# One encoder layer in emulated fp32: output and down projections with stationary weights and features on partitions

## The chip, the core and the metric

The kernel is written in Bass with the Tile framework and runs on one core of a Trainium2 chip. The time is device microseconds of one execution; the profile is one execution taken by the hardware profiler.

A core has five engines with instruction queues of their own: PE (matrix products; its weight loads are counted apart as PEld), DVE, ACT and POOL (elementwise work) and SP (here it only issues transfers). An engine takes its instructions in order and waits for semaphores of the others. Transfers between DRAM and the on-chip memory run on 16 DMA engines. On-chip tiles have 128 partitions. PE multiplies a stationary operand of at most 128 x 128 by a moving operand and writes into PSUM; "128x272" behind a matmul is its output, 128 partitions by 272 moving columns.

## What is computed

One inference step of one layer: 1024 prompt frames and 64 sample frames, each with 1024 features. The two parts share all weights, so the kernel treats them as T = 1088 tokens.

```python
def trunk(x, ...):
    m = mixer(rmsnorm(x, g_mix), ...)       # projection, conv and attention, gates, w_out
    x = x + m
    x = x + swiglu(rmsnorm(x, g_ffn), w_ff1, w_ff3, w_ff2)
    return rmsnorm(x, g_final)

def mixer(xn, ...):
    cb, cc, ch, q, k, v, ga, gb = split(xn @ w_in)      # 1024 x 5120
    ya = (cb * conv3(cc * ch)) @ w_conv_out
    yb = band_attention(q, k, v) @ w_attn_out
    return (sigmoid(ga) * ya + sigmoid(gb) * yb) @ w_out   # 1024 x 1024

def swiglu(x, w1, w3, w2):                  # 1024 x 2816, twice, then 2816 x 1024
    return (silu(x @ w1) * (x @ w3)) @ w2

def rmsnorm(x, g):                          # over the features of a token
    return x * rsqrt(mean(x * x) + 1e-6) * g
```

## The kernel before

**Numbers.** An fp32 operand is held as two parts of PE's fast fp32 type: `hi`, a cast on ACT, and `lo = x - hi` on DVE (`split`, lines 152 and 153). A product of two operands is three matmuls: hi·hi, hi·lo, lo·hi.

**Seven products.** The input projection, the up-projection (w_ff1 and w_ff3) and the down-projection (w_ff2) use a seven-product scheme of 2 x 2 blocks. The moving operand is kept as seven tiles 1 to 7, each a block of tokens and features or a sum of blocks (class `Seven`). `first` builds tiles 1 and 2 from the first token half; `second` builds 3 to 7 from the second half and from what was kept of the first. `both` is a split, `minus` a difference on DVE (line 160). The products run in the order `STEPS = [1, 2, 6, 7, 5, 4, 3]`. A `Unit` is 256 columns of a weight; `prep(step)` makes its part on ACT and DVE, `step_of` (`sa_step`, `sb_step` for the first two units) issues the products of one step.

**Columns.** A half is HT = 544 token columns (512 prompt tokens and 32 sample frames), HN = 272 is half of that. In the layouts with features on partitions the columns are prompt tokens 0 to 511, 32 sample frames, prompt tokens 512 to 1023, 32 sample frames.

**Stages.** V projection (0 to 78 us), the rest of the input projection (to 373), attention and gates (to 573), merge of the two branches (to 671), output projection (to about 782), up-projection (to 1239), down-projection (to 1473), end. The Tile framework schedules each engine's list ahead of time from the program and its dependences; a pool's buffers come free tile by tile, and `tc.issue_after` sets an instruction behind another.

**Output projection** (lines 1061 to 1225). The merged input `mg` has features on partitions, in four tiles of half the features by half the tokens (tiles 1 to 4 of the up-projection later overwrite it). In `token_product` 128 tokens of `mg` are stationary and 512 columns of w_out move, so that tokens come out on partitions: 8 groups of 128 prompt tokens, and the 64 sample frames, which have a copy `ms` with hi and lo side by side. The first output half (`wo_hi`, `wo_lo`) adds the residual, stores the sums x1 and x1 times g_ffn, and takes the row sum of squares from ACT's accumulation. The second half (`second`) goes in `ORDER = [8, 0, 4, 1, 5, 2, 3, 6, 7]`: add, square, a factor of one column (`norm_factor`, lines 162 to 171: scale, Sqrt, reciprocal, a Newton step), two scaled halves (the first half read back, on ACT; the second on DVE, L1174). `turned` (L1176) transposes the token group on PE, in eight 128 x 128 pieces, and calls `xf.first` or `xf.second`. It runs one group late; the last group's stands between the up-projection's first steps.

**Hidden layer** (`hidden_done`). The product silu(a)·b is split into hi and lo and stored in seven tiles (`h_d`); its sample frames go apart (`hs_d`).

**Down-projection** (lines 1268 to 1590). 128 tokens of a hidden tile are stationary (`ht`), 512 columns of w_ff2 move from a ring of prepared weights (`Down`, `W2`, `ring_of`). The hidden features go in four blocks (KB = 2, 3, 3, 3 pairs of tiles), within one two token groups g, seven steps, two pieces j. PSUM tags: A, two buffers of one bank; BD, four of one. The 64 sample frames are multiplied without the scheme, in `frames`, into PSUM of their own (`ys`). In the last block the residual is added, and `half_ended` (L1468) works per 128 tokens: squares with accumulation, `norm_factor`, two scaled halves with a row of g_final (`gfb`; L1490), stores of 128 tokens by 512 features by SP and ACT.

Of the kernel before, what the change touches and what calls it, by code (L numbers as in the profile page):

```python
# [15 lines left out]
P = 128  # L16
# [26 lines left out]
def spots(a, n):  # L43


    edges = [(0, 512, 0), (512, 1024, 544)]
    r = []
    for lo, hi, at in edges:
        s, e = max(a, lo), min(a + n, hi)
        if s < e:  # L50
            r.append((s - a, at + s - lo, e - s))
    return r
# [42 lines left out]
def encoder_kernel(ctx: ExitStack, tc: tile.TileContext, ins, outs):  # L95
# [23 lines left out]
    cols = const.tile([P, 20], F32, name="cols")  # L119
    nc.scalar.dma_start(cols, ins["cols"])  # L120
    gm = cols[:, 12:20]
# [4 lines left out]
    x1_d = dr.tile([T, D], F32, name="x1_d")  # L126
    y0_d = dr.tile([T, 512], F32, name="y0_d")
    h_d = dr.tile([NF // 2, 7, P, 4 * 2 * P], F32, name="h_d")
    hs_d = dr.tile([NF // 2, P, 2, 2 * TS], F32, name="hs_d")
# [43 lines left out]
    class Seven:  # L173
# [5 lines left out]
        def first(self, src, c, n, kept=None):  # L179
            for g in range(2):  # L180
                both(self.t[1 + g], c, n, src[g])
                if kept is not None:
                    act.copy(kept[:, g], src[g])

        def second(self, src, c, n, kept, f):
            t = self.t
            both(t[3], c, n, src[1])
            minus(f[:, 0], src[0], kept[:, 0])
            minus(f[:, 1], src[1], f[:, 0])
            both(t[6], c, n, f[:, 1])  # L190
# [70 lines left out]
    def bank2(tag, nm):  # L261
        return stage["ps"].tile([P, 2, 512], F32, tag=tag, name=nm, bufs=2 if tag == "A" else 1)
# [112 lines left out]
    HORDER = [0, 1, 2, 8, 4, 3, 5, 6, 7]  # L375
    with tc.tile_pool(name="ph", bufs=2, reuse_waits="tile") as ph:
        xts, xns, pls = {}, {}, {}

        def load_x(i):
# [3 lines left out]
            xt = xts[i] = ph.tile([P, KD, P], F32, tag="xt", name=f"xt{i}", bufs=6)  # L383
# [47 lines left out]
        def formed(i):  # L431
# [8 lines left out]
            if i == 8:  # L440
# [96 lines left out]
    def conv_units(cvp, c2):  # L537
# [44 lines left out]
        def cb_done(r, h, src, snap):  # L582
# [4 lines left out]
            for a, t, n in places(h):  # L587
                nc.gpsimd.dma_start(u_d[i * P : (i + 1) * P, t : t + n], x[:, a : a + n])
# [6 lines left out]
    def cache_tile(hp):  # L595
        ct = cp.tile([P, CACHE], F32, tag="ct", name=f"ct{hp}")
# [108 lines left out]
    gp = pool_of("gp", 3, stack=t_stack)  # L705
# [14 lines left out]
    def gate_chunk(n, c, behind=None):  # L720
# [74 lines left out]
    def row_sums(h):  # L795
# [8 lines left out]
        nc.gpsimd.dma_start(r_d[h, :TP].rearrange("(a p) -> a p", p=P), rr[:8])  # L804
        nc.gpsimd.dma_start(r_d[h : h + 1, TP:], rr[8:9, :TS])

    def combine(h, pv, n, tok, nm):
# [7 lines left out]
        nc.gpsimd.dma_start(o_d[h * HD : (h + 1) * HD, tok : tok + n], o[:, :n])  # L815
# [148 lines left out]
    pm_stack.close()  # L964
    o_stack.close()
# [13 lines left out]
    ms = mspool.tile([P, KD, 2, TS], F32R, tag="ms", name="ms")  # L979
# [27 lines left out]
    with tc.tile_pool(name="mgp", bufs=3, reuse_waits="tile") as mp:  # L1007
        for m0 in range(0, 8, 2):
            for j in range(2):
# [26 lines left out]
                def joined(c):  # L1036
# [5 lines left out]
                    if o + n > TP:  # L1042
                        split(ms[:, m, 0, :], ms[:, m, 1, :], t[:, TP - o : n])
# [13 lines left out]
    t_stack.close()  # L1057
# [568 lines left out]
```

## Time and profile before

| what | value |
|---|---|
| median of three runs | 1484.99 us (1484.95 to 1487.14) |
| the profiled execution | 1482.88 us, its span 1481.1 us |
| mean granted PE clock | 0.998 |
| read from and written to DRAM | 170.56 MB and 87.62 MB, 174 GB/s |
| matmuls on PE in windows: input projection (78 to 373 us) | 2326 |
| merge and output projection (573 to 782 us) | 1115 |
| up-projection (782 to 1239 us) | 3652 |
| down-projection (1239 to 1473 us) | 1036 |

The span runs from the first to the last instruction; the execution's own time has 1.8 us more. The page gives busy time of each engine, the span in slices, the chain of work that ended last, and groups of instructions by source line. In a group's row stand line, engine and operation, output<-inputs, shape, count, then busy us and mean ns of one, then idle time of the engine ahead of them and what ended most of it. Matmuls overlap in the array, so that a group's mean is longer than the time from one start to the next. In the views by windows a row has the stretch, its length, busy time (and count) of PE, PEld, DVE, ACT and POOL, the granted clock, the share of time that the DMA engines were busy, and GB/s.

### The profile page before, as it was taken

The page shows a single profiled execution, that of the slowest core. Times are in us where ns is not written, and L with a number is a line of the kernel's source. Part 1 is how long each engine was busy: PE and PEld are TensorE (multiplying, and loading weights), DVE is VectorE, ACT ScalarE, POOL GpSimd, SP SyncE. Part 2 cuts the span into 40 slices and gives each one's busy share as a digit, 9 for nine tenths or more (in the row PEclk, how much of TensorE's full clock was granted, in tenths as well). Part 3 has the DMA queues.
Part 4 walks back from the last instruction along what each step waited for, and adds up shares of the span by engine and source line. Part 5 has one row for each costly group of instructions (what it writes and reads, how often), then busy time and mean ns, then how long its engine had stood idle before and what let it go on. Part 6 is the DMA issues. An engine that isn't in the chain of part 4 may idle for free.

```text
span 1481.1 us, 25804 instructions
## 1 busy us (share of the span) xinstructions
PE 1460.2 (99%) x9864; PEld 1366.2 (92%) x9864; DVE 1001.7 (68%) x1962; ACT 680.2 (46%) x1383; POOL 198.1 (13%) x347
## 2 busy tenths in 40 slices
PE   8999999999999999999999999999999999999997
PEld 6799999999999999998889999999999999888886
DVE  7976565653577776755688667766666667957676
ACT  6544332322677775642465444444344445512223
POOL 0344221122122221001100111111001111000000
PEclk9999999999999999999999999999999999999999
DMA  9666332346766627636533444343334448867675
GB/s 312 197 225 216 133 63 85 65 133 202 209 172 176 172 79 214 204 116 224 167 97 124 154 153 148 145 160 124 114 127 161 146 171 302 305 210 248 207 265 201
DMA packets 144876, 256.48 MB, mean 173 GB/s; under 512 B 20288, under 2 KB 84096, under 8 KB 144608
## 3 DMA queue, kind: packets, MB, share of 16 engines
q1 hardware_dynamic: 116720, 169.56, 37.2%
q0 software_dynamic: 26736, 83.17, 15.7%
q10 hardware_dynamic: 1296, 2.11, 0.4%
q8 instruction: 77, 1.26, 0.4%
q14 instruction: 47, 0.39, 0.1%
HBM read 170.56 MB, written 87.62 MB: 174 GB/s over the span
## 4 chain that ended last, share of the span: by engine, by line
PE 94%; DVE 2%; ACT 2%; DMA 1%; issue 1%; POOL 0%; SPq 0%; ACTq 0%; DVEq 0%; POOLq 0%
PE Aa L285 9%; PE Ab L285 9%; PE A L1541 8%; PE Db L285 4%; PE Da L285 4%; PE D L1541 4%; PE Ag L285 3%; PE p L701 2%; PE p L699 2%; PE p L700 2%; PE t L863 2%; PE Bb L285 2%; PE Ba L285 2%; PE B L1541 2%; PE wo L1078 2%; PE wo L1079 2%
## 5 line engine op out<-in xcount | busy, mean ns | idle before, releaser
L1541 PE MATMUL A<-ring,ht 128*128 128x512 f32 x528 | 124.4, 390 | 0.0
L1541 PEld LDWEIGHTS A<-ring,ht 128*128 128x128 f32 x528 | 99.0, 188 | 21.1 <-ACT acc L1551 0.2
L1261 POOL DMA_DIRECT2D h_d<-hq x77 | 41.1, 534 | 406.7 <-DVE hq L153 207.8
L152 ACT CAST ring<-w2r 128x512 fp32r<-128x512 f32 (+1 forms) x78 | 43.2, 588 | 88.6 <-PE A L1541 42.7
L152 ACT CAST hq<-sa 128x512 fp32r<-128x512 f32 x77 | 47.8, 621 | 75.0 <-DVE sa L1273 56.8
L153 DVE TENSOR_TENSOR wla<-rawa,wha 128x512 fp32r<-128x512 f32 x55 | 37.8, 688 | 42.7 <-ACT wha L152 42.7
L153 DVE TENSOR_TENSOR hq<-sa,hq 128x512 fp32r<-128x512 f32 x77 | 53.0, 689 | 20.0 <-ACT hq L152 19.9
L1541 PE MATMUL D<-ring,ht 128*128 128x512 f32 x264 | 63.4, 392 | 0.0
L1541 PEld LDWEIGHTS D<-ring,ht 128*128 128x128 f32 x264 | 49.6, 188 | 11.1
L783 DVE CUSTOM_DVE_ANT_0 p<-s,bias 128x640 f32<-128x640 f32 (+5 forms) x72 | 47.4, 659 | 17.3 <-PE s L833 17.2
L285 PE MATMUL Aa<-tt,wha 128*128 128x272 f32 x352 | 58.8, 288 | 0.1
L285 PE MATMUL Ab<-tt,whb 128*128 128x272 f32 x352 | 58.6, 287 | 0.0
L285 PE MATMUL Ab<-mg,whb 128*128 128x272 f32 x352 | 58.4, 288 | 0.0
L285 PE MATMUL Aa<-mg,wha 128*128 128x272 f32 x352 | 58.4, 288 | 0.0
L152 ACT CAST wha<-rawa 128x512 fp32r<-128x512 f32 x55 | 33.9, 621 | 51.3 <-PE Ab L285 36.0
L701 PE MATMUL p<-xo,wlp 128*128 128x272 f32 x192 | 57.0, 297 | 0.0
L700 PE MATMUL p<-xo,whp 128*128 128x272 f32 x192 | 56.4, 294 | 0.0
L699 PE MATMUL p<-xo,whp 128*128 128x272 f32 x192 | 56.2, 293 | 0.0
L153 DVE TENSOR_TENSOR ring<-w2r,ring 128x512 fp32r<-128x512 f32 (+1 forms) x78 | 48.4, 647 | 11.3 <-ACT ring L152 11.3
L793 ACT ACTIVATE p<-p,mx 128x640 f32<-128x640 f32 (+5 forms) x72 | 50.9, 706 | 9.2 <-DVE mx L783 8.7
L152 ACT CAST whb<-rawb 128x512 fp32r<-128x512 f32 x55 | 34.0, 620 | 39.4 <-PE Aa L285 26.8
L1553 DVE TENSOR_TENSOR acc<-A,acc 128x512 f32<-128x512 f32 x52 | 35.7, 687 | 23.3 <-PE A L1541 22.9
(523 smaller groups left out, 4557.7 us busy)
## 6 DMA issues: line engine op xcount, KB each, us to landing
h_d<-hq POOLq DMA_DIRECT2D x77, 512.0 KB, 3.8
ht<-h_d SPq DMA_DIRECT2D x154, 256.0 KB, 3.5
rawa<-in_w_ff SPq DMA_DIRECT2D x11, 1024.0 KB, 6.0
rawb<-in_w_ff SPq DMA_DIRECT2D x11, 1024.0 KB, 5.2
w2r<-in_w_ff SPq DMA_DIRECT2D x11, 1024.0 KB, 7.1
qd<-q_d SPq DMA_DIRECT2D x32, 272.0 KB, 5.5
xn<-in_x_prompt SPq DMA_DIRECT2D x8, 512.0 KB, 6.7
xt<-in_xt SPq DMA_DIRECT2D x8, 512.0 KB, 6.1
```

The costliest lines, as they stand in the source:

```text
L152: c = act.copy(hi, src)
L153: vec.tensor_tensor(lo, src, hi.bitcast(F32), op=ALU.subtract)
L285: mm(t[:, j, :HN], x[:, k, :], moving(p, l, k, j * HN, HN), start=p in (1, 2, 7) and k == 0 and n == 0, stop=k == 3 and n == 2, skip_group ...
L699: mm(out, a, p, start=g == 0 and k == 0, stop=False)
L700: mm(out, a, q, start=False, stop=False)
L701: mm(out, b, p, start=False, stop=g == last and k == 3)
L783: vec.tensor_tensor_reduce(out=s if len(ps.shape) == 2 else s.rearrange("p (a b) -> p a b", a=2), in0=ps, in1=bias if len(ps.shape) == 2 e ...
L793: act.activation(s, s, AF.Exp, bias=mx, scale=-1.0, accum_out=sm)
L863: nc.tensor.transpose(tp[:, i * P : (i + 1) * P], s[:, i * P : (i + 1) * P], ident)
L1261: nc.gpsimd.dma_start(h_d[p, c - 1], hq.rearrange("p i l t -> p (i l t)").bitcast(F32))
L1541: mm(t, ht[k][:, j, x], w[:, l], start=p in (1, 2, 7) and k == 0 and n == 0, stop=k == len(ks) - 1 and n == 2, skip_group_check=p in (6, 5 ...
L1553: behind["DVE"] = vec.tensor_tensor(o, t, o, op=ALU.add).ins
```

## The change

Tokens no longer come out on partitions anywhere.

**Output projection.** `projected(hf, c)` takes one output half hf and one of four chunks c of 272 token columns; weights are stationary (128 x 128), `mg` moves, and 128 features by 272 tokens come out. Chunks 0 and 1 are the first token half. `PASS` sets the order: 0, 1, 2, 3 for the first output half, 0, 2, 1, 3 for the second. Squares are taken by ACT with features on partitions, added on DVE, and summed over partitions by an f32 product with a matrix of -0.5 (`rows2`), which leaves the same row on all partitions. `row_factors` turns that 128 x 272 row into factors with the operations that were done on one column before. The scaling multiplies by a column of g_ffn and by that row, 272 columns at a time. The sums x1 are stored features first and the first half of them is read back (`half_load`); the input x comes transposed from the host's copy. There are no transposes, no `y0_d`, no `ms`. The seven tiles are built in pieces of 272 instead of 128 columns; `both` is at lines 149 and 150 and `minus` at 157 now.

**Down-projection.** Weights are stationary, `ht` moves 272 columns; the sample frames are in the columns, so `frames`, `hs_d` and `ys` go. PSUM: A and BD have two buffers of two banks. `ended` replaces `half_ended`: squares are added up over the four pieces of a chunk, summed by a product with -0.5, turned into factors, and eight scaled products and four stores per chunk follow. The output leaves as one array `y`, features by 1088 columns, and the host takes it apart. The residual's rows are loaded into free parts of the weight ring.

**Elsewhere.** Gates, conv outputs, attention outputs and their factors are stored in the 1088-column order, so a piece of 544 goes with one store where two went. The merge's pieces split at columns 544 instead of 512. The tile order at the start (`HORDER`) goes from 0, 1, 2, 8, 4, 3, 5, 6, 7 to 0, 1, 4, 2, 5, 8, 3, 6, 7; the buffers of `xt` from 6 to 5 and of `ct` to 1; one pool moves to the other side of memory. In the up-projection's first two units the steps stand in another order (below), and their PSUM for B and D has two buffers instead of one.

```diff
+    def projected(hf, c, weights):
...
+        for mp in range(2):
+            t = bank2("A", f"wo{hf}{c}{mp}")
+            for j in range(2):
+                w = slice((2 * mp + j) * P, (2 * mp + j + 1) * P)
+                for k in range(KD):
+                    wh, wl = weights(k)
+                    for n, (a, l) in enumerate(((wh, 0), (wh, 1), (wl, 0))):
+                        mm(
+                            t[:, j, :HN], a[:, w], mg.at(l, k, c * HN, HN),
...
+            y = x[:, 2 * mp : 2 * mp + 2]
+            added = vec.tensor_tensor(y, t[:, :, :HN], y, op=ALU.add).ins
+            squared = act.activation((q, r)[mp], y, AF.Square).ins
...
+        rows = bank2("BD", f"rows2_{c}")[:, 0, :HN]
+        mm(rows, minus_half, q[:, 0], start=True, stop=True)
...
+    def row_factors(pool, rows, nm):
...
+        vec.tensor_scalar(v, rows, -2.0 / D, EPS, op0=ALU.mult, op1=ALU.add)
+        act.activation(y, v, AF.Sqrt)
+        vec.reciprocal(y, y)
+        act.activation(z, y, AF.Square)
+        vec.tensor_tensor(z, z, v, op=ALU.mult)
+        vec.scalar_tensor_tensor(z, z, -3.0, y, op0=ALU.add, op1=ALU.mult)
...
+    def second(n):
+        c = PASS[1][n]
...
+        x, rows = projected(1, c, lambda k: w2[k])
+        r = row_factors(wp, rows, f"f{c}")
+        src = [first_x.pop(c), x]
+        for g in range(2):
+            for m in range(4):
+                y = src[g][:, m]
+                at = 4 * g + m
+                vec.scalar_tensor_tensor(y, y, g_neg[:, at : at + 1], r, op0=ALU.mult, op1=ALU.mult)
+        if c < 2:
+            kept[c] = src
+            xf.first(src, c * HN, HN)
+        else:
+            xf.second(src, (c - 2) * HN, HN, kept.pop(c - 2), src)
...
     sa_step(0)
     sa_step(1)
-    turned(*last)
...
     sb_step(0)
     sb_step(1)
+    sa_step(2)
     for si in range(2, len(STEPS)):
+        ub.prep(si)
+    sb_step(2)
+    for si in range(3, len(STEPS)):
         sa_step(si)
-        ub.prep(si)
+    for si in range(3, len(STEPS)):
+        sb_step(si)
...
+                    for j in range(2):
+                        c = slice((2 * jp + j) * P, (2 * jp + j + 1) * P)
+                        for k, kp in enumerate(ks):
+                            w = W2[kp].w[p]
+                            for n, (l, x) in enumerate(((0, 0), (0, 1), (1, 0))):
+                                mm(
+                                    t[:, j, :HN], w[:, l, c], ht[k][:, x],
```

In the whole program PE's matmuls go from 9857 to 10962: those of 272 columns from 6816 to 9443, those of 512 from 1750 to 324. DVE's instructions go from 1964 to 1863, ACT's from 1278 to 1156.

The first place is the end of the output projection on PE. Before, the last token group's 512-column products (`wo_7`) are followed by another group's transposes and the first step of the up-projection (`Aa`; `wha` and `wla` are the parts of its weights, `mg_7065` is tile 1):

```order
L1077 MATMUL wo_7_8939<-woh_7_8423,mg_7068 128x512
L1078 MATMUL wo_7_8939<-wol_7_8424,mg_7068 128x512
L1079 MATMUL wo_7_8939<-woh_7_8423,mg_7068 128x512
L1191 MATMUL xt_6_8976<-ident,xg_6_8878 128x128 x8
L285 MATMUL Aa_9011<-mg_7065,wha_1_8461 128x272 x4
L285 MATMUL Aa_9011<-mg_7065,wla_1_8462 128x272 x2
L285 MATMUL Aa_9011<-mg_7065,wha_1_8461 128x272 x4
L285 MATMUL Aa_9011<-mg_7065,wla_1_8462 128x272 x2
```

Now the last chunk's products of 272 columns are followed by the product over partitions of the chunk ahead of it, and then by the up-projection's first products on tile 1 (`mg_7032`), which alternate between the first unit (`Aa`) and the second (`Ab`):

```order
L1125 MATMUL wo_9016<-mg_7035,woh_7_8535 128x272 x2
L1125 MATMUL wo_9016<-mg_7035,wol_7_8536 128x272
L1142 MATMUL rows_1_8940<-q_8832,minus_half 128x272
L280 MATMUL Aa_9113<-mg_7032,wha_1_8546 128x272
L280 MATMUL Ab_9196<-mg_7032,whb_1_9105 128x272
L280 MATMUL Aa_9113<-mg_7032,wha_1_8546 128x272 x2
L280 MATMUL Ab_9196<-mg_7032,whb_1_9105 128x272 x2
L280 MATMUL Aa_9113<-mg_7032,wha_1_8546 128x272
L280 MATMUL Aa_9113<-mg_7032,wla_1_8547 128x272 x2
```

So no transposes stand between them any more, and the up-projection's first step comes behind two chunks of which the last has no row product yet.

The second place is DVE in the second output half. Before, between the add-back of one token group (`wo_5`) and its scaled product stand the lo parts and sums of an earlier group, in pieces of 512 elements, and factors of one column:

```order
L1095 TENSOR_TENSOR x_5_8701<-wo_5_8703,x_5_8701 128x512
L153 TENSOR_TENSOR tt_8456<-left_8627,tt_8456 128x4x128
L153 TENSOR_TENSOR mg_7067<-left_8627,mg_7067 128x4x128
L166 TENSOR_SCALAR normf_8732<-ssq_5_8730,more 128x1
L153 TENSOR_TENSOR mg_7065<-xt_1_8740,mg_7065 128x4x128
L168 RECIPROCAL normf_8732<-normf_8732 128x1
L169 SCALAR_TENSOR_TENSOR normf_8732<-normf_8732 128x1
L170 SCALAR_TENSOR_TENSOR normf_8732<-normf_8732 128x1
L1174 SCALAR_TENSOR_TENSOR xg_5_8699<-x_5_8701,normf_8732,gb_row 128x512
```

Now the factors of chunk 2 (`x_12`) stand around the first of the add-backs of chunk 1's second output half (`x_11`, from `wo_8834` and `wo_8885`), then come eight scaled products, and the sums and lo parts of chunk 2, of 1088 elements (`mg_7035` is tile 3, `tt_8540` tile 5):

```order
L1074 TENSOR_SCALAR factorf_8801<-rows_2_8799 128x272
L1076 RECIPROCAL factorf_8801<-factorf_8801 128x272
L1130 TENSOR_TENSOR x_11_8554<-wo_8834,x_11_8554 128x544
L1078 TENSOR_TENSOR factorf_8801<-factorf_8801 128x272
L1079 SCALAR_TENSOR_TENSOR factorf_8801<-factorf_8801 128x272
L1180 SCALAR_TENSOR_TENSOR h_8689<-h_8689,g_neg,factorf_8801 128x272 x4
L1180 SCALAR_TENSOR_TENSOR x_12_8422<-x_12_8422,g_neg,factorf_8801 128x272 x4
L157 TENSOR_TENSOR h_8689<-h_8689,h_8556 128x1088
L1130 TENSOR_TENSOR x_11_8554<-wo_8885,x_11_8554 128x544
L150 TENSOR_TENSOR mg_7035<-x_12_8422,mg_7035 128x4x272
L150 TENSOR_TENSOR tt_8540<-h_8689,tt_8540 128x4x272
L157 TENSOR_TENSOR x_12_8422<-x_12_8422,h_8689 128x1088
```

The factors of chunk 1 come only behind all of these rows; chunk 1's half of tile 1, which the up-projection's first step reads, is made with them.

The third place is the end of DVE's list. Before, the last add-back from PSUM (`A_3`) is followed by factors of one column and a scaled product of 512 elements for one token group, and by the same for another:

```order
L1553 TENSOR_TENSOR acc_1_14422<-A_3_16074,acc_1_14422 128x512
L166 TENSOR_SCALAR normy_16265<-ssq_0_16263,more_16250 128x1
L168 RECIPROCAL normy_16265<-normy_16265 128x1
L169 SCALAR_TENSOR_TENSOR normy_16265<-normy_16265 128x1
L170 SCALAR_TENSOR_TENSOR normy_16265<-normy_16265 128x1
L1490 SCALAR_TENSOR_TENSOR acc_0_14420<-acc_0_14420,normy_16265,gfb 128x512
L166 TENSOR_SCALAR normy_16287<-ssq_1_16285,more_16154 128x1
L168 RECIPROCAL normy_16287<-normy_16287 128x1
L169 SCALAR_TENSOR_TENSOR normy_16287<-normy_16287 128x1
L170 SCALAR_TENSOR_TENSOR normy_16287<-normy_16287 128x1
```

Now the last add-back (`A_11`) stands within the factors of one chunk, and the factors of the last chunk follow behind eight scaled products:

```order
L1444 RECIPROCAL last_raw<-last_raw 128x272
L1520 TENSOR_TENSOR acc_14389<-A_11_16666,acc_14389 128x544
L1446 TENSOR_TENSOR last_raw<-last_raw 128x272
L1447 SCALAR_TENSOR_TENSOR last_raw<-last_raw 128x272
L1453 SCALAR_TENSOR_TENSOR acc_14387<-acc_14387,g_out,last_raw 128x272 x4
L1453 SCALAR_TENSOR_TENSOR acc_14388<-acc_14388,g_out,last_raw 128x272 x4
L1442 TENSOR_SCALAR last_raw<-rows_10_16972 128x272
L1444 RECIPROCAL last_raw<-last_raw 128x272
L1446 TENSOR_TENSOR last_raw<-last_raw 128x272
L1447 SCALAR_TENSOR_TENSOR last_raw<-last_raw 128x272
L1453 SCALAR_TENSOR_TENSOR acc_14385<-acc_14385,g_out,last_raw 128x272 x2
L1453 SCALAR_TENSOR_TENSOR acc_14386<-acc_14386,g_out,last_raw 128x272 x2
```

Behind the last add-back stand four small operations per group and one wide one before; now two full rows of 272, one of them with its reciprocal still to come, and sixteen scaled products.

More of the change, by code (lines that the diff above doesn't have):

```diff
@@ L1101, in x_rows @@
-    def x_rows(i):
-        t0, n = TT[i]
-        return x_p[t0 : t0 + n] if t0 < TP else x_s
+    stage["ps"], stage["BD"] = psA, 2
+    def row_factors(pool, rows, nm):
+        three = pool.tile([P, 3, HN], F32, tag="factor", name=f"factor{nm}", bufs=1)
+        v, y, z = (three[:, i] for i in range(3))
+        vec.tensor_scalar(v, rows, -2.0 / D, EPS, op0=ALU.mult, op1=ALU.add)
[4 more added lines that the diff above has]
+        vec.scalar_tensor_tensor(z, z, -3.0, y, op0=ALU.add, op1=ALU.mult)
+        return z
@@ new lines, in encoder_kernel, with chunk, x_load @@
+    squares = mspool.tile([P, T], F32, tag="ms", name="squares")
+    def chunk(c):
+        return slice(c * HN, (c + 1) * HN)
+    def x_load(hf, c):
+        x = wp.tile([P, 4, HN], F32, tag="x1", name=f"x1_{hf}{c}", bufs=4)
+        return x, nc.sync.dma_start(
+            x, ins["xt"][hf * 512 : (hf + 1) * 512, chunk(c)].rearrange("(m p) t -> p m t", p=P)
+        ).ins
+    PASS = [[0, 1, 2, 3], [0, 2, 1, 3]]
+    ahead = [(hf, c) for hf in range(2) for c in PASS[hf]]
+    xts = {}
+    for key in ahead[:2]:
+        xts[key], x_last = x_load(*key)
@@ new lines, in encoder_kernel @@
+    for n, c in enumerate(PASS[0]):
+        for key in ahead[n + 2 : n + 3]:
+            xts[key], _ = x_load(*key)
+        added, squared = projected(0, c, lambda k: (wo_hi[:, k], wo_lo[:, k]))
+        with tc.issue_after(added), tc.issue_after(squared):
+            w2_prep(2 * n)
+            w2_prep(2 * n + 1)
+    tt = {7: tpool.tile([P, 2, 4, HT], F32R, tag="o7", name="tt7")}
+    tt[5] = tpool.tile([P, 2, 4, HT], F32R, tag="o5", name="tt5")
+    tt[6] = t6pool.tile([P, 2, 4, HT], F32R, tag="o6", name="tt6")
@@ L1223, in encoder_kernel @@
+    ua = Unit(ins["w_ff1"][0][:, : 2 * P], "a0")
+    ua.pool = wp
+    ua.prep(0)
+    ua.prep(1)
+    ua.pool = ws
+    for n in range(4):
+        second(n)
     stage["x"] = xf
@@ L1464, in encoder_kernel @@
         if n < len(homes):
             pool, tag = homes[n]
[L1466 removed]
+            acc[key] = pool.tile([P, 2, HN], F32, tag=tag, name=nm, bufs=bufs[pool, tag])
         elif n % 2 == 0:
[L1468 to L1471 removed]
@@ L1473, in encoder_kernel @@
[L1473 to L1491 removed]
+            two = hp.tile([P, 2, 2, HN], F32, tag="hq", name=nm, bufs=6)
```

459 lines of the change are left out of this document (172 added, 287 removed).

## The prediction

> **What bounds the kernel now.** I read the page first: the busy shares, then the chain that ended last.
>
> ```profile
> span 1481.1 us, 25804 instructions
> PE 1460.2 (99%) x9864; PEld 1366.2 (92%) x9864; DVE 1001.7 (68%) x1962; ACT 680.2 (46%) x1383; POOL 198.1 (13%) x347
> PE 94%; DVE 2%; ACT 2%; DMA 1%; issue 1%; POOL 0%; SPq 0%; ACTq 0%; DVEq 0%; POOLq 0%
> ```
>
> PE is busy for 99% of the span and is 94% of the chain. So the time is the number of matmuls by the time from one start to the next, plus what PE waits, plus the tail behind the last matmul. Matmuls overlap, so a mean duration is no price; I take windows in which PE does one thing. Columns: stretch, its us, then busy us (and instructions) of PE, PEld, DVE, ACT, POOL, granted clock, DMA share, GB/s.
>
> ```profile
> 788.00:1218.00 430.00, 429.89 (x3436) 429.49 (x3435) 289.65 (x487) 192.31 (x361) 44.05 (x82) 1.00 0.40 143
> 723.50:775.20 51.70, 51.70 (x257) 42.46 (x256) 40.00 (x95) 32.86 (x75) 4.79 (x9) 1.00 0.40 125
> 1239.00:1473.00 234.00, 233.61 (x1036) 192.22 (x1034) 167.22 (x298) 74.47 (x148) 3.21 (x6) 1.00 0.73 249
> ```
>
> First row: the up-projection, all 272 columns: 430.00/3436 = **125 ns** a matmul, each with its own weight load. Second: most of the second half of the output projection, without a PE gap. Third: the down-projection, 234 us. The timeline of PE gives the 512-column price and the ends of the stages (columns: start us, us until the last one ends).
>
> ```profile
> 670.98 0.63 PE L1077 MATMUL wo<-wo_hi,mg 128*128 128x512 f32 x2
> ...
> 775.26 0.75 PE L285 MATMUL Aa<-mg,wha 128*128 128x272 f32 x4
> ...
> 781.39 1.04 PE L1191 MATMUL xt<-ident,xg 128*128 128x128 f32 x8
> ...
> 1439.60 8.32 PE L1541 MATMUL A<-ring,ht 128*128 128x512 f32 x36
> 1447.76 4.24 PE L1541 MATMUL B<-ring,ht 128*128 128x512 f32 x18
> ...
> 1470.64 1.98 PE L1541 MATMUL A<-ring,ht 128*128 128x512 f32 x8
> ```
>
> 36 matmuls from 1439.60 to 1447.76: **227 ns** each, and this for 512 columns. Two pieces of 272 cost 250 ns: 6% more columns, 10% more time. The output projection takes PE from 670.98 to 775.26, and one group of its transposes (1.04 us) stands later: 105 us. The last matmul ends at 1472.6; the tail to 1481.1 is 8.5 us.
>
> **The PE terms.** Output projection: 416 matmuls of 512 and 72 transposes go; 2 x 4 x 4 x 8 x 3 = 768 of 272 come, 768 x 0.125 = 96.1 us. Four products over partitions come too, in plain f32. Their nearest rows:
>
> ```profile
> L425 PE MATMUL rows<-diag,minus_half 128*128 128x128 f32 x16 | 3.3, 308 | 1.1 <-DVE diag L423 1.1
> L1191 PE MATMUL xt<-ident,xg 128*128 128x128 f32 x64 | 8.3, 273 | 0.0
> ```
>
> Eight f32 products leave 16 records, so each is two passes; eight passes of 128 columns take 1.04 us at 781.39 (0.11 each). 272 columns twice are then 0.46 us, four 1.9. With about 1 us of first wait as before: 99 against 105, **-6 us**. Down-projection: 924 matmuls of 512 and 110 for the sample frames go, 1848 x 0.125 = 231.2 us come, and three row products 1.4: 232.6 against 234.0, **-1 us**. So PE's own work hardly shrinks, and the answer lies in waits.
>
> **The wait behind the output projection.** Before, DVE had 40.00 us of work in 51.70 us of PE, and its last 128-token piece is small. Now the second half works in four chunks of 272 tokens, in the order 0, 2, 1, 3, and each chunk ends in a chain on DVE. Prices, from rows (groups: count, busy us, mean ns):
>
> ```profile
> 565.69 2.49 DVE L153 TENSOR_TENSOR u<-u 128x1088 fp32r<-128x1088 f32 x2
> L153 DVE TENSOR_TENSOR u<-u 128x1088 fp32r<-128x1088 f32 x4 | 4.9, 1287 | 1.5 <-ACT u L152 1.5
> L1273 DVE TENSOR_TENSOR sa<-sb,sa 128x544 f32<-128x544 f32 x22 | 15.8, 719 | 0.0
> L1034 DVE TENSOR_TENSOR ga<-yga,ga 128x320 f32<-128x320 f32 x8 | 3.9, 486 | 0.3 <-ACT ga L1026 0.3
> L427 DVE SCALAR_TENSOR_TENSOR xt<-xt,cols,rows 128x128 f32<-128x128 f32 x64 | 17.8, 343 | 2.8 <-PE rows L425 2.8
> L1490 DVE SCALAR_TENSOR_TENSOR acc<-acc,normy,gfb 128x512 f32<-128x512 f32 x8 | 6.0, 750 | 0.3
> L799 DVE RECIPROCAL rc<-rs 128x9 f32<-128x9 f32 x8 | 1.6, 205 | 1.0 <-ACT p L793 1.0
> L168 DVE RECIPROCAL normf<-normf 128x1 f32<-128x1 f32 x8 | 1.2, 156 | 0.3 <-ACT normf L167 0.3
> L728 ACT COPY gst<-p 128x272 f32<-128x272 f32 x32 | 12.3, 383 | 13.2 <-PE p L701 13.1
> ```
>
> Two operations of 1287 ns end after 2.49: the next starts 0.08 before the end. So 1088 elements cost DVE 1.20 us, 544 cost 0.64, 272 (between 320 at 486 ns and less) 0.36, and a scaled product of 272 with a column of factors, between 343 and 750 ns, 0.41. The reciprocal of a 272-wide row is not in the trace. Nine columns take 49 ns more than one, 6 ns an element, which gives 1.7 us; if the rest were as cheap as in a product it would be 0.36. I take **1.7**, since its own two rows say so, and keep both.
>
> The Trainium skill, page "VectorE: DVE Perf Modes", section "Walkthrough: the 8-slice pipeline in each mode", says that a reciprocal runs an iterative divide repeated eight times. Eight times the 1.06 ns an element between the two product rows would be 2.3 us, an estimate, and the whole sum about 4 us more; the 6 ns of the rows lie nearer to it than to one pass.
>
> A chunk's head on DVE: two add-backs and a sum at 0.64, two sums of 0.36, then 0.36 + 1.7 + 0.36 + 0.41, then eight scaled products, 3.3: 8.7 us. Chunks 0 and 1 add two split halves (2.4), chunk 2 adds nine operations of 1088 (10.8). PE gives a chunk 96 x 0.125 = 12.0 us. The up-projection's first product reads tile 1 in both chunks of a half, so its second column piece needs chunk 1, which DVE reaches only behind the 10.8 us of chunk 2. DVE begins with chunk 0 at 12.9 us (all counted from the half's start on PE): 11.1 + 19.5 + 8.7 + 1.2, two weight splits of 0.6, and about 6 us of handing to ACT (a 272-wide ACT operation is 0.38 us, two in a row per chunk) and to PE bring it to about 61. PE has done its four chunks and row products by 50.5. First wait: **10 us**. PE then has 96 matmuls of the products 1 and 2, 12.0 us, and wants tile 6. For that DVE does the split of chunk 1's second half (1.2), chunk 3's head (8.7, of which its two add-backs, 1.3, are done already), six operations of 1088 (7.2), seven of weights (4.2) and an add (0.6): about 21 us, to 82. PE would be there at 72 to 73: second wait **10 us**. Together **+20**. With the cheap reciprocal and every ACT hand-over hidden 5 and 3 fewer: 12. With hand-overs twice as long: 24.
>
> **The clock.** A wait of 10 us is longer than any that the trace has inside, but the trace shows what the clock does behind the last matmul and at the start:
>
> ```profile
> 1473.00:1475.00 2.00, 0.00 (x0) 0.00 (x0) 1.62 (x6) 1.44 (x4) 0.00 (x0) 1.00 0.68 262
> 1475.00:1477.00 2.00, 0.00 (x0) 0.00 (x0) 1.46 (x6) 0.88 (x3) 0.00 (x0) 0.62 0.48 188
> 1477.00:1479.00 2.00, 0.00 (x0) 0.00 (x0) 0.18 (x1) 0.15 (x1) 0.00 (x0) 0.50 0.67 259
> L409 PE MATMUL wake<-zero 128*128 128x512 f32 x11 | 5.1, 643 | 1.6 <-DVE zero L406 1.6
> ```
>
> The granted clock falls to a half some 3 us after PE stops, and the 11 matmuls at the start take 5.1 us, about 0.43 each, twice 0.227. So PE comes out of each wait at half speed. After the first wait this delays the row product of chunk 3, which stands behind some twenty matmuls, by 2.5 us; after the second it costs half of the time at half speed. I take **+4**, from 0 to 9.
>
> The Trainium skill, page "TensorE: Matmul & The Clock Gate", section "Why this matters for your kernels", warns of idle gaps over about 3 us, after which the clock drops. The trace agrees (0.62, then 0.50). By its window of 3.4 us each restart costs about 1.7 us, an estimate, 3.4 together; the sum would be 1 us less.
>
> **The tail.** The rows of before's end:
>
> ```profile
> 1476.43 0.75 DVE L1490 SCALAR_TENSOR_TENSOR acc<-acc,normy,gfb 128x512 f32<-128x512 f32 x1
> ...
> 1477.18 0.37 ACTq L1489 DMA_DIRECT2D out_y_prompt<-acc  x1
> ```
>
> From the last store's issue to the end are 3.9 us; the stores keep their size, so this stays. Before, a token's factor was one column and the last half needed five small operations and one of 512. Now two chunks end within one step: behind the last matmul stand on DVE the reciprocal of chunk 3 (1.5 left), an add-back (0.64), 0.36 + 0.41, eight scaled products (3.3), then for chunk 1 again 0.36 + 1.7 + 0.36 + 0.41 + 3.3, with two ACT hand-overs of 0.5 in this part: 13.4, and 3.9: 17.3 against 8.5, **+9**; with cheap reciprocals +6, with another 2 us of hand-overs +11. Nothing covers it: PE has no work left.
>
> **The start.** The tile order there puts the dear second-half tiles earlier; PE then starves between them and keeps a backlog for the end. In before it has little idle time there:
>
> ```profile
> 0.00:78.00 78.00, 71.74 (x324) 56.20 (x325) 65.69 (x194) 45.69 (x92) 15.54 (x25) 1.00 0.81 249
> ```
>
> DVE (65.69 of 78 us) sets this stage's pace, and its work is the same; I take **+1**, from -1 to +3. The fewer stores on POOL's queue and the undivided pieces of the merge shorten work off PE's path (POOL 13% busy): 0. The up-projection keeps its matmuls: 0, covered by DVE's spare 140 us of 430 there.
>
> **Sum.** -6 - 1 + 20 + 4 + 9 + 1 = **+27 us**, on the profiled execution's 1482.88 (span 1481.1 and 1.8 around it) 1510. The median of the runs shown is 1484.99, 2 us above that; the same difference gives **1512**.
>
> **Rivals.**
> - *Short waits.* If reciprocals cost like products and ACT's part is hidden, the waits are 12, the clock hardly falls (+1), the tail is +6: -6 - 1 + 12 + 1 + 6 + 1 = +13, **1498**. For: the price of a wide reciprocal rests on two narrow rows. Against: 6 ns an element between these rows.
> - *Long waits.* ACT's queue also holds the casts of tiles and weights; if the factors wait behind them, 24 + 9 + 11 + 3 - 7 = +40, **1525**.
> - *PE never waits.* The place is the start of the up-projection, the price the 20 + 4 us; it decides if tile 6 is ready when PE arrives, that is if DVE's list is 20 us shorter than I add. Then -7 + 6 = -1, **1484**, or with an end as short as before's -7, **1478**, faster. Against it: 1088 elements at 1.20 us are measured, and there are some 22 of them behind the first chunk's scaling.
> - *The weight loads of short pieces are not hidden.* Each 272-column matmul would cost more than 125 ns; but the up-projection loads weights for each and runs at 125. Not counted.
>
> **Chances.** Forecast (1503 to 1518) 0.58, short waits (1490 to 1503) 0.20, long waits (1518 to 1535) 0.14, PE never waits 0.08, half of it faster. A measurement of this kernel can tell about 0.2%, 3 us, from no change; so faster 0.05, same 0.03, slower 0.92. The range takes both neighbours in nearly to their ends: **1494 to 1528**.
>
> **What would show it.** Right: PE idle twice, some 10 us each, between the last matmul of the output projection and tile 6's product, ended by DVE (tiles mg and tt), with a granted clock below 1.00 behind; reciprocals of 272 near 1.8 us; 272-column matmuls of the down-projection 125 ns apart, about 232 us in all; 17 us behind the last matmul. Wrong: no such PE gap, or a 272-wide reciprocal of 0.4 us; a down-projection far from 232 us would break the PE terms.

## The result and the profile after

The changed kernel takes **1524.41 us** (median of 4 runs, 1521.37 to 1526.02) against 1484.97 before (1484.54 to 1487.14): a ratio of 1.026, 95% interval 1.024 to 1.0281, 39 us slower. The forecast was 1512 with a range of 1494 to 1528. The two profiled executions, 1482.88 and 1526.02 us, lie 43 us apart and not 39, since the second is the longest of its four.

The page of the changed kernel, its span, its busy shares, and the chain that ended last:

```profile
span 1524.2 us, 27616 instructions
PE 1470.9 (97%) x10980; PEld 1430.5 (94%) x10980; DVE 1020.1 (67%) x1861; ACT 647.9 (43%) x1226; POOL 166.0 (11%) x285
PE 77%; DVE 5%; issue 3%; DMA 3%; ACT 1%; POOL 0%; SPq 0%; DVEq 0%; ACTq 0%; POOLq 0%
```

PE is busy for only 10.7 us longer than before, and the span grew by 43.1. So most of the loss is waiting, and PE's share of the chain fell from 94% to 77%. Where it is, one sees by cutting both spans at the same events on PE: the first key product, the first conv product, the start of the merge, of the output, up- and down-projection, and the last matmul. Before, by windows:

```profile
0.00:75.28 75.28, 69.02 (x302) 53.49 (x303) 63.55 (x191) 44.33 (x90) 15.05 (x24) 1.00 0.83 253
75.28:155.98 80.70, 78.95 (x626) 78.32 (x624) 54.89 (x85) 38.92 (x68) 34.42 (x53) 1.00 0.64 218
155.98:573.10 417.12, 415.35 (x3146) 399.55 (x3145) 262.30 (x569) 208.88 (x455) 84.56 (x152) 1.00 0.51 139
...
670.98:775.26 104.28, 103.57 (x483) 84.32 (x481) 67.36 (x145) 46.98 (x107) 14.09 (x26) 1.00 0.51 172
775.26:1239.05 463.79, 463.68 (x3708) 463.28 (x3706) 318.79 (x539) 212.67 (x400) 45.65 (x85) 1.00 0.41 148
1239.05:1472.60 233.55, 233.55 (x1036) 192.17 (x1034) 166.82 (x297) 74.17 (x148) 3.21 (x6) 1.00 0.73 250
1472.60:1481.10 8.50, 0.01 (x1) 0.00 (x0) 3.61 (x11) 2.71 (x7) 0.00 (x0) 0.67 0.48 186
```

After, at the same events:

```profile
0.00:82.50 82.50, 71.88 (x302) 53.60 (x303) 64.94 (x193) 44.85 (x90) 15.07 (x24) 0.96 0.76 227
82.50:168.73 86.23, 81.31 (x625) 80.88 (x624) 53.19 (x82) 38.55 (x67) 34.36 (x53) 0.96 0.62 208
168.73:585.84 417.11, 415.08 (x3146) 399.63 (x3145) 262.10 (x569) 208.69 (x455) 67.73 (x121) 1.00 0.51 139
...
683.68:785.74 102.06, 99.71 (x777) 97.72 (x775) 57.59 (x89) 26.76 (x39) 5.30 (x7) 1.00 0.42 140
785.74:1270.94 485.20, 470.31 (x3699) 468.99 (x3699) 339.90 (x520) 214.52 (x359) 40.36 (x75) 0.98 0.41 144
1270.94:1506.90 235.96, 234.38 (x1857) 233.31 (x1856) 166.17 (x263) 61.97 (x107) 2.66 (x5) 1.00 0.73 249
1506.90:1524.20 17.30, 2.09 (x8) 1.07 (x7) 12.54 (x24) 1.95 (x4) 0.00 (x0) 0.67 0.38 129
```

Row by row: start +7.2, first units of the input projection +5.5, the rest and the merge 0.0, output projection -2.2, up-projection +21.4, down-projection +2.4, tail +8.8. The sum is 43.1. The first two were forecast at +1 together. Output and up-projection together (+19.2 against +18) and the tail (+8.8 against +9) come near the forecast; the down-projection was forecast at -1.

What PE waits for at the start of the up-projection (engine, line waited for, us in total, times, longest):

```profile
PE Aa L280 <- ACT tt L149: 6.4, 1, 6.4
PE Aa L280 <- ACT mg L149: 6.1, 1, 6.1
PE rows L1142 <- DVE q L1140: 1.7, 1, 1.7
PE Da L280 <- ACT tt L149: 1.0, 1, 1.0
PE Ab L280 <- DVE x L1130: 0.9, 1, 0.9
```

These are the two forecast waits: for tile 1 (mg) and for tile 6 (tt). ACT ends them with a cast, but the casts stand behind DVE's scaling and, for tile 6, its differences. DVE's groups of that stretch give the prices that the forecast had to work out:

```profile
L1076 DVE RECIPROCAL factorf<-factorf 128x272 f32<-128x272 f32 x4 | 7.4, 1850 | 2.4 <-ACT factorf L1075 2.4
L1180 DVE SCALAR_TENSOR_TENSOR h<-h,g_neg,factorf 128x272 f32<-128x272 f32 x16 | 7.0, 498 | 0.1
```

The wide reciprocal takes 1.85 us (forecast 1.7), and a scaled product 0.50 by its record, 0.41 from start to start (four in 1.65), as forecast. The granted clock behind the waits:

```profile
794.00:796.00 2.00, 1.56 (x7) 1.24 (x6) 2.00 (x2) 1.65 (x2) 0.00 (x0) 0.50 0.03 8
818.00:820.00 2.00, 2.00 (x11) 2.00 (x11) 2.00 (x3) 1.10 (x1) 0.00 (x0) 0.50 0.00 0
```

At a clock of 0.50 a matmul of 272 columns comes every 0.227 us; some 24 do so behind each wait, which is 2.4 us each.

At the start, one wait of ACT and one of PE (same columns):

```profile
ACT stq L340 <- DMA out_cache_v_prompt<-vst: 3.8, 1, 3.8
...
PE Aq L280 <- ACT whq L149: 4.9, 1, 4.9
```

ACT's cast of the first query tile (`stq`) waits until 90.16 us for the store of a V tile (`vst`). Behind it stand DVE's part of that tile and its sums of weights, the casts of the next weights (`whq`) and PE, which stands still from 88.7 to 93.6. Before, it waits 1.0 us here. The two tiles have nothing to do with each other but their place. Byte ranges per partition in the two compiled programs:

```
         V tile buffers (vst)   first query tile (stq)
before   52512 to 56608         48160 to 52512
after    48480 to 52576         48224 to 52576
```

Before, the ranges touch and do not overlap. The V stage's pool has five input buffers `xt` (4096 bytes) instead of six, so all behind them moved down by 4032 (the gains took 64). The sixth no longer fits: with it the pool needs 53.125 KB, and 51.625 are left, since each of the 16 input buffers that the down-projection shares grew from 2048 to 2176 bytes, 512 to 544 columns.

### The profile page after: what moved, and what is told of

The parts are those of the page before. It is cut to its first block, busy times and chain, and to the rows that moved or that the text cites. A ratio compares the mean times of both kernels' runs of the same rounds, so it can differ in the third digit from the quotient of the medians.

```text
span 1524.2 us, 27616 instructions
## 1 busy us (share of the span) xinstructions
PE 1470.9 (97%) x10980; PEld 1430.5 (94%) x10980; DVE 1020.1 (67%) x1861; ACT 647.9 (43%) x1226; POOL 166.0 (11%) x285
## 4 chain that ended last, share of the span: by engine, by line
PE 77%; DVE 5%; issue 3%; DMA 3%; ACT 1%; POOL 0%; SPq 0%; DVEq 0%; ACTq 0%; POOLq 0%
PE Aa L280 9%; PE Ab L280 8%; PE A L1508 7%; PE wo L1125 5%; PE Da L280 4%; PE Db L280 4%; PE D L1508 4%; PE t L867 2%; PE Ba L280 2%; PE B L1508 2%; PE Bb L280 2%; PE p L694 2%; PE p L692 2%; PE p L693 2%; PE pv L893 2%
## 5 line engine op out<-in xcount | busy, mean ns | idle before, releaser
L1508 PE MATMUL A<-ht,ring 128*128 128x272 f32 x1056 | 138.2, 289 | 1.3 <-ACT acc L1518 1.3
L1508 PEld LDWEIGHTS A<-ht,ring 128*128 128x128 f32 x1056 | 134.6, 188 | 1.9 <-ACT acc L1518 1.5
L149 ACT CAST hq<-sa 128x544 fp32r<-128x544 f32 x77 | 49.8, 647 | 80.5 <-DVE sa L1245 56.8
L149 ACT CAST ring<-w2r 128x512 fp32r<-128x512 f32 x66 | 38.1, 621 | 100.4 <-PE A L1508 59.6
L150 DVE TENSOR_TENSOR hq<-sa,hq 128x544 fp32r<-128x544 f32 x77 | 55.5, 721 | 20.9 <-ACT hq L149 20.7
L1508 PE MATMUL D<-ht,ring 128*128 128x272 f32 x528 | 68.8, 288 | 0.0
L1508 PEld LDWEIGHTS D<-ht,ring 128*128 128x128 f32 x528 | 67.2, 188 | 0.0
L280 PEld LDWEIGHTS Aa<-mg,wha 128*128 128x128 f32 x352 | 51.4, 193 | 7.6 <-ACT mg L149 6.3
L280 PEld LDWEIGHTS Aa<-tt,wha 128*128 128x128 f32 x352 | 51.7, 194 | 6.7 <-ACT tt L149 6.7
L150 DVE TENSOR_TENSOR ring<-w2r,ring 128x512 fp32r<-128x512 f32 x66 | 44.2, 685 | 19.4 <-ACT ring L149 19.3
```

The costliest lines, as they stand in the source:

```text
L149: c = act.copy(hi, src)
L150: vec.tensor_tensor(lo, src, hi.bitcast(F32), op=ALU.subtract)
L280: mm(t[:, j, :HN], x[:, k, :], moving(p, l, k, j * HN, HN), start=p in (1, 2, 7) and k == 0 and n == 0, stop=k == 3 and n == 2, skip_group ...
L1508: mm(t[:, j, :HN], w[:, l, c], ht[k][:, x], start=p in (1, 2, 7) and k == 0 and n == 0, stop=k == len(ks) - 1 and n == 2, skip_group_check ...
```

## The experiments

All were timed beside the kernel before, on the same chip within each group. Before took 1484.69 us beside s1 to s4, 1484.25 beside s5 to s8, and 1486.00 beside s9 and s10, which ran on another chip than the base s3; so for these two the distance to before is given as well. Stage lengths below are from each run's profiled execution, between the first matmuls of the stages; "tail" starts at the last matmul on weights. A stage's length differs between executions without any edit: s9 has the lists of s3 up to the output projection, and its first key product comes 4.3 us later; s4 has the lists of before from the first key units on, and its merge is 2.5 and its down-projection 1.6 us longer. So a few us in one row of one execution prove nothing.

| run | median us | first key product at | first conv product at | output proj. | up | down | tail |
|---|---|---|---|---|---|---|---|
| before | 1484.97 | 75.3 | 156.0 | 104.3 | 463.8 | 233.2 | 8.9 |
| changed | 1524.41 | 82.5 | 168.7 | 102.1 | 485.2 | 235.7 | 17.6 |
| s1 old order | 1521.84 | 75.8 | 165.3 | 102.1 | 485.4 | 235.0 | 17.6 |
| s2 moved buffers | 1516.75 | 79.8 | 160.6 | 102.1 | 484.0 | 235.4 | 17.6 |
| s3 both (the base) | 1513.46 | 76.3 | 157.1 | 102.1 | 484.6 | 235.3 | 17.6 |
| s4 before, new order | 1491.43 | 81.2 | 161.9 | 104.5 | 463.8 | 234.8 | 8.8 |
| s5 chunks 0, 1, 2, 3 | 1513.78 | 76.5 | 157.3 | 100.4 | 486.2 | 235.0 | 17.7 |
| s6 part on POOL | 1522.31 | 77.1 | 158.0 | 112.2 | 482.9 | 235.5 | 17.7 |
| s7 no reciprocal | 1506.31 | 77.6 | 158.5 | 100.6 | 482.1 | 236.8 | 14.9 |
| s8 clock held | 1513.75 | 77.1 | 158.0 | 102.1 | 481.3 | 237.3 | 17.7 |
| s9 less on DVE | 1511.23 | 80.6 | 161.5 | 100.6 | 481.8 | 235.3 | 17.7 |
| s10 one function | 1509.96 | 76.8 | 157.6 | 99.9 | 482.1 | 240.1 | 14.2 |

### The start: order and place (s1 to s4)

Theory: the new tile order and the shifted buffers each cost a part. Rival: one cause, the lost sixth buffer, and all else follows from it.

```diff
s1:
-    HORDER = [0, 1, 4, 2, 5, 8, 3, 6, 7]
+    HORDER = [0, 1, 2, 8, 4, 3, 5, 6, 7]
s2:
-        zero = ph.tile([P, ATT], F32R, tag="vst", name="zero")
+        zero = ph.tile([P, 2 * ATT], F32R, tag="pl", name="zero")[:, :ATT]
s4, in the kernel before:
-    HORDER = [0, 1, 2, 8, 4, 3, 5, 6, 7]
+    HORDER = [0, 1, 4, 2, 5, 8, 3, 6, 7]
```

> The changed kernel with only the tile order of the start put back to 0, 1, 2, 8, 4, 3, 5, 6, 7; the five buffers of the transposed input stay. In the trace of the changed kernel the first product of the first key unit starts at 82.50 us, before at 75.28: 7.2 us later, with PE waiting between V tiles. Theory (the order sets this): about 7 us less, 1517 us, while the wait of 5.2 us at 88.4 us stays. Rival (the lost sixth buffer sets it, the order only adapts to it): loads wait for buffers instead, within 2 us of the changed kernel's 1524.

> The changed kernel with only one tile moved: the zero tile of the start takes a buffer of the tag of pl, so that the V tiles' store buffers lie elsewhere in memory and the first query tile no longer lies over the last of them. No engine's list of instructions changes. Theory (ACT at 90.16 us waits for the store of the last V tile out of memory that the query tile takes over, and PE behind it): the gap of 5.2 us at 88.4 us shrinks to the 1.3 us of before and the clock stays, 5.5 us less, 1519 us. Rival (the wait is put down to the store only because it ends last; the V stage's lateness sets it): within 2 us of 1524.

> Both edits on the changed kernel: old tile order and moved store buffers. If the two pieces are separate, 7.2 + 5.5 = 12.7 us less, 1511 to 1512 us, which is the predicted time, and the merge starts near 573 us instead of 585.8. If they are one and the same lateness, no less than the better of the two alone, 1517.

> The kernel before with only the new tile order 0, 1, 4, 2, 5, 8, 3, 6, 7 and its six buffers. Theory (order): 6 to 8 us more, 1491 to 1493 us. Rival (the order is harmless, five buffers do the harm): within 2 us of 1485.

**s4** shows that the order counts: it alone, with six buffers, makes the kernel before 6.7 us slower (1491.43 against 1484.69 beside it, ratio 1.0046, interval 1.0031 to 1.0061, which is 4.6 to 9.1 us). Nothing but the order of the tiles is changed in it. **s2** settles the place: the lists of all engines are those of the changed kernel, the V buffers now lie at 57824 to 61920, and what PE waits for at the query weights fell to what it was before:

```profile
PE Aq L280 <- ACT whq L149: 1.0, 1, 1.0
```

It gained 7.7 us, 2.2 more than expected; by the table 2.7 us of that stand ahead of this wait. The runs do not say why; it is less than the 4.3 us by which s9 and s3 differ at this point with the same lists. **s1** gained 2.6 instead of 7: the first key product comes 6.7 us earlier, as the theory had it, but then ACT waits for the same store, and PE for longer, so that 3.4 are left at the first conv product:

```profile
ACT stq L340 <- DMA out_cache_v_prompt<-vst: 7.0, 1, 7.0
...
PE Aq L280 <- ACT whq L149: 8.1, 1, 8.1
```

**s3**, with both, gains 11.0 us, where 12.7 were expected. So the two are separate causes, and they nearly add up: on the changed kernel the order gives 2.6 us with the bad place (s1) and 3.3 with the good one (s2 to s3), the place 7.7 in the new order and 8.4 in the old. Why the order costs twice as much in the kernel before (s4) stays open. With both mended the first conv product comes at 157.1 to 158.5 us in s3, s5 to s8 and s10 (161.5 in s9), against 156.0 before: five buffers in the old order cost 1 to 2.5 us by that mark, so the rival falls. What is left, 1513.46, is 1.5 us above the forecast.

### The waits at the start of the up-projection (s5 to s10, on the base s3)

Theory A, the prediction's: DVE's list is the bound there. Theory B: the bound is the chain of the last chunk alone, from its row product over factors and scaling to the cast.

```diff
s5:
-    PASS = [[0, 1, 2, 3], [0, 2, 1, 3]]
+    PASS = [[0, 1, 2, 3], [0, 1, 2, 3]]
...
-        first_x[c] = wp.tile([P, 4, HN], F32, tag="h", name=f"h{c}")
+        first_x[c] = wp.tile([P, 4, HN], F32, tag="h", name=f"h{c}", bufs=3)
s6, for chunk 2 (e is POOL; in s9 the first line goes to ACT as a copy, the differences go):
-            both(t[3], c, n, src[1])
+            e.tensor_tensor(t[3][:, 1, :, c : c + n], src[1], ..., op=ALU.subtract)
-            minus(kept[0], f[1], kept[0])
+            e.tensor_tensor(kept[0], f[1], kept[0], op=ALU.subtract)
s7:
-        vec.reciprocal(y, y)
+        vec.tensor_scalar_mul(y, y, 1.0)
s8:
+            with tc.issue_after(row_sum):
+                for i in range(28):
+                    mm(bank[:, 1], w2[7][0][:, :P], w2[7][0], start=True, stop=True)
s10:
-        act.activation(y, v, AF.Sqrt)
-        vec.reciprocal(y, y)
+        act.activation(y, v, AF.Abs_reciprocal_sqrt)
```

> Base: the changed kernel with old tile order and moved store buffers (1513.5 us; PE starts products of the up-projection at 773.6, waits to 782, and from 796.6 to 804.9). Here the second output half takes its chunks in the order 0, 1, 2, 3, with a third buffer for the first half read back. Theory (the wait for tile 1 is the last chunk-1 chain of row product, factors and scaling, about 8.5 us from the row product on; it would lie beside two chunks of matmuls): no first wait, one wait for tile 6 of 10 to 14 us, one restart at half clock instead of two: 5 to 7 us less, 1507. Rival (DVE's list is the bound, its length is the same, so the waits only move): within 2 us of the base.

> The same base; five of the nine wide operations on chunk 2 (lo parts of tiles 3, 7 and 4 and two differences, 6.0 us of DVE) go to POOL, which is idle there. Theory of the prediction (DVE reaches chunk 1 only behind chunk 2's work): first wait 5 to 6 us shorter, 1508. Rival (what PE waits for is the chain of chunk 1 itself; DVE's backlog only delays its row product, by 1.9 us): 2 us less, 1511 to 1512. If POOL is over three times slower than DVE, products 7, 5 and 4 wait for it and the time rises.

> The same base with the reciprocals of the eight factor rows left out: a product with 1.0 of the same shape stands in their place, so the factors are wrong. It takes 0.4 instead of 1.85 us, 1.4 less each. Theory (they lie on the chains that PE and the end wait for): 1.4 less in each of the two waits and in each of the last two chunks, 5.6 us in all, 7 with chunk 2's: 1506 to 1508. Rival (hand-overs and wide operations set the waits, the reciprocals lie beside them): only the end's 2.8, 1510.7.

> The same base with 28 matmuls without use in PE's first wait and 30 in the second (512 columns, 6.4 and 6.8 us), so that the granted clock stays at 1.00 behind them. In the base some 24 matmuls behind each wait take 0.227 instead of 0.125 us, 2.4 us each. Theory (a restart's cost ahead of another wait is hidden by that wait, since DVE sets its end): only the second counts, 2 to 3.5 us less, 1510 to 1511.5. Rival (both count): 5 less, 1508.5. Rival (the dummies' own time delays the row product of chunk 3 or the first real product): no gain or some loss.

**s5** speaks for A: 1513.78 against 1513.46, no change. The wait for tile 1 is gone, and PE waits 10 us at the next thing that DVE must do, chunk 3's row product:

```profile
PE rows L1142 <- DVE q L1140: 10.1, 1, 10.1
PE Aa L280 <- ACT tt L149: 5.9, 1, 5.9
```

DVE runs without a pause from 769.4 to 811.4 us in this trace, so the waits only move.

**s7** gained 7.2 us for 1.4 us in each row, as much as five of the eight rows in full; in its profile output and up-projection give 4.0, the tail 2.7. The forecast gave the tail 3 us for it.

**s6** lost 8.9 us. The five operations take POOL 2.6 to 3.5 us each, and DVE's own slow down while POOL runs. DVE's rows, and one of POOL at the same time:

```profile
766.54 3.04 DVE L1140 TENSOR_TENSOR q<-q,q 128x544 f32<-128x544 f32 x1
769.51 3.56 DVE L150 TENSOR_TENSOR tt<-x,tt 128x1088 fp32r<-128x1088 f32 x1
772.99 2.71 DVE L1144 TENSOR_TENSOR q<-q 128x272 f32<-128x272 f32 x1
...
765.52 3.48 POOL L191 TENSOR_TENSOR h<-x,h 128x1088 f32<-128x1088 f32 x1 [0.69 <-DVE x L157]
```

The same operations take 0.72, 1.28 and 0.44 us in the changed kernel. The Trainium skill, page "SBUF — State Buffer", section "Who interferes with whom", says that tensor_tensor with both inputs in on-chip memory contends with POOL's reads; the trace agrees, with a DVE operation 2.3 us longer. s6 therefore did not test A against B; s9 does it without POOL.

**s8** kept the clock at 1.00 through both waits:

```profile
782.00:784.00 2.00, 1.56 (x9) 1.12 (x8) 2.00 (x6) 1.10 (x1) 0.00 (x0) 1.00 0.00 0
806.00:812.00 6.00, 6.00 (x48) 6.00 (x49) 6.00 (x8) 2.35 (x3) 0.00 (x0) 1.00 0.00 0
```

The up-projection is 3.3 us shorter in the profile, as expected, but the time is the same, 1513.75: the merge (1.4 us) and the down-projection (2.0) are longer in that execution. s4 shows such differences in stages that its edit leaves alone; whether these answer to the edit stays open, and with it what the slow clock costs the whole.

> The base (old tile order, moved store buffers; 1513.5 us). Five wide operations of DVE on chunk 2 are left out (two differences, and the lo parts of tiles 3, 7 and 4, which ACT fills with a copy instead); the values are wrong by that. It takes 6.0 us from DVE's list and gives POOL nothing to do. Theory (DVE's list from chunk 2 to tile 6 sets the sum of PE's two waits): 5 to 6 us less, 1508. Rival (the chain of the last chunk itself sets them): 2 us less or nothing, 1511.5 to 1513.5.

> The base with ACT's function for one over the square root in place of its Sqrt and DVE's reciprocal, in all eight factor rows; the Newton step stays. Each chain loses 1.85 us on DVE and one hand-over. With the reciprocals at 0.4 us the base fell by 7.1 us; at five counted rows and 2.0 us each it falls by 10: 1503 to 1504. If the function needs table loads of its own (1.28 us for the one of Sqrt ahead of chunk 0) between the chunks, two or three of them come back: 1506 to 1507.

**s9** took 6.0 us off DVE's list and gained 2.2, or 3.5 by the distance to before: between the two theories. In its profile output and up-projection are 4.3 us shorter together. What PE waits for:

```profile
PE Aa L294 <- ACT tt L149: 6.4, 1, 6.4
PE Aa L294 <- ACT mg L149: 3.3, 1, 3.3
...
PE rows L1156 <- DVE q L1154: 0.2, 1, 0.2
```

The first wait loses 2.8 us and the row product's 1.4; the second keeps its 6.4. DVE now waits for row products (0.82 and 1.65 us before two of the factor chains), and chunk 3's row product stands on PE behind the first wait. From there DVE works without a pause to the difference that tile 6 is cast from, in s9 as in the base:

```profile
788.16 0.44 DVE L1088 TENSOR_SCALAR factorf<-rows 128x272 f32<-128x272 f32 x1 [1.65 <-PE rows L1156]
...
801.66 1.28 DVE L157 TENSOR_TENSOR x<-x,h 128x1088 f32<-128x1088 f32 x1
```

These 14.7 us (14.6 in the base) are chunk 3's chain and some 6 us of other work: weights, an add-back, the lo parts of tiles 3 and 5. So A holds for the first wait, by about two thirds of the 6 us. The second is set behind chunk 3's row product, whatever DVE did ahead of it; there the chain and DVE's list run together, and no run takes the other work out, so A and B are not separated for it.

**s10** keeps the results and gained 3.5 us, or 4.8 by the distance to before, instead of 10. Output and up-projection give 4.6 and the tail 3.4; no table load comes back. But the down-projection is 4.9 longer. PE waits there for two sums of squares of the final norm (in the base it waits for none), and then runs at half clock for some 3 us; the waits (2.2 us) and that clock (1.7) make about 3.9 of the 4.9, an estimate. DVE and PE in s10:

```profile
1460.08 3.38 DVE L1451 SCALAR_TENSOR_TENSOR acc<-acc,g_out,last_raw 128x272 f32<-128x272 f32 x8
1463.38 0.43 DVE L1436 TENSOR_TENSOR sums_raw<-sums_raw 128x272 f32<-128x272 f32 x1
...
1455.13 0.70 PE L1439 MATMUL rows<-sums_raw,minus_half 128*128 128x272 f32 x2 [0.43 <-DVE sums_raw L1436]
1463.87 0.73 PE L1439 MATMUL rows<-sums_raw,minus_half 128*128 128x272 f32 x2 [1.79 <-DVE sums_raw L1436]
1464.23 2.04 PE L1506 MATMUL B<-ht,ring 128*128 128x272 f32 x8
```

With the factor ready earlier, the eight scaled products of one chunk stand ahead of the next chunk's sum in DVE's list; in the base the sum comes first (1464.04, ahead of 1465.38). s10 is the fastest that gives the reference's results, 14 us faster than the changed kernel, and still 1.66% slower than before (interval 1.42% to 1.89%).

## Why the prediction came out as it did

- **The time: within the range, but not for a reason that the prediction names.** 1524.41 lies 12 us above the forecast, in the stretch that was left to the long waits (1518 to 1535, chance 0.14). Those did not come: waits and clock measure 21.3 us against 24 forecast and 33 by that rival. The start brought the time there, which no rival mentions; that the range was wide enough for it is in part luck.
- **The start: wrong, and with it the size of the whole.** The step was "DVE (65.69 of 78 us) sets this stage's pace, and its work is the same; I take +1, from -1 to +3." It measured +12.7. DVE's work is the same (63.55 and 64.94 us), so equal work did not mean equal time. The order costs 6.7 us in the kernel before (s4) and 2.6 to 3.3 in the changed one. The buffer count does not appear in the prediction's sum; by s2 it moved a buffer under another tile, which costs 7.7 to 8.4. Both together are 11.0 us by the times (s3). The 11.7 us between +12.7 and +1 are most of the 16 between the forecast's 1510 for a profiled execution and the 1526.02 measured.
- **The waits: right in place, near in size.** Forecast 10 and 10 with +4 of clock. PE waits 16.5 us (the list above and one of 0.4), and 48 slow matmuls cost 4.8. The mechanism needs a correction: the forecast added up DVE's list in one piece. DVE's backlog sets the first wait only in part, and it does not reach the second, which starts anew at chunk 3's row product (s9). The rival that PE never waits is refuted by the rows; of the short and the long waits neither is nearer than the forecast.
- **The wide reciprocal: right.** 1.7 against 1.85 us. The estimate of 2.3, from the Trainium skill, page "VectorE: DVE Perf Modes", section "Walkthrough: the 8-slice pipeline in each mode", was too long; the extrapolated narrow rows came nearer. s7 shows that it counts.
- **Output projection: -2.2 instead of -6,** in part because the forecast counted PE's wait for a row product (1.7 us) and the pause behind it among the 20. With the up-projection the two make +19.2 against +18.
- **Down-projection: +2.4 instead of -1.** 1848 matmuls at 0.125 came near the forecast (a mean of 0.1256, some 0.9 us in all). The rest, as far as the trace shows it, is one pause of 1.6 us at 1313 for a PSUM buffer, and row products of 0.7 us each where 0.46 were taken. The pause need not belong to the change: s4, with the down-projection of before, has one of 1.7 us at 1291.
- **Tail: right.** +9 forecast, +8.8 measured, in the forecast order: add-back, eight scaled products, a whole second chain. The rows of the second chain:

```profile
1512.95 0.43 DVE L1442 TENSOR_SCALAR last_raw<-rows 128x272 f32<-128x272 f32 x1
1514.01 1.85 DVE L1444 RECIPROCAL last_raw<-last_raw 128x272 f32<-128x272 f32 x1 [0.62 <-ACT last_raw L1443]
1516.36 0.44 DVE L1446 TENSOR_TENSOR last_raw<-last_raw 128x272 f32<-128x272 f32 x1 [0.50 <-ACT last_raw L1445]
1516.83 0.44 DVE L1447 SCALAR_TENSOR_TENSOR last_raw<-last_raw 128x272 f32<-128x272 f32 x1
1517.31 3.39 DVE L1453 SCALAR_TENSOR_TENSOR acc<-acc,g_out,last_raw 128x272 f32<-128x272 f32 x8
```

## What to carry to other kernels

A change of layout is paid far from where it is made: count the bytes of every buffer that grows, see which pool then loses one, and look at what lies on what afterwards; a tile can wait for the store of another with which it shares nothing but the place. The reciprocal of a full 128 x 272 row took 1.85 us, where that of a column took 0.16, and it lies bare wherever the next product needs the last tokens. Before work is moved off a full engine, see where its list starts anew behind a wait: s9 took off 6 us and gained 2 to 4.

## What the runs showed that was not expected

POOL and DVE on two-input operations at the same time slow each other: POOL took 2.6 to 3.5 us for 1088 elements, and DVE's 272 wide sum 2.71 instead of 0.44. And the clock fell behind waits much shorter than the 10 us of the forecast: in s10 PE idled 0.43 and 1.79 us within 10 us, and then ran at half clock for some 3 us:

```profile
1465.00:1467.00 2.00, 2.00 (x11) 2.00 (x11) 1.58 (x4) 0.86 (x2) 0.00 (x0) 0.50 1.09 360
```

In the changed kernel the clock fell twice at the start, too, the second time behind a wait of 2.6 us that ended at 51.7 (mean clock 0.83 from 50 to 60 us); but a wait of 1.6 us at 1313 us was followed by one slow matmul only. What decides it the runs do not show.
